# Moving the load of the norm factors ahead on ScalarE's DMA queue, and the first weight tile to SP's

## The chip, the cores and the metric

The kernel runs on one core of a Trainium2 chip. The time is that of the device, in microseconds (us), from several executions; each kernel is also profiled once, and the profile covers the span from the first to the last instruction of that execution.

The engines appear by the profile's names: PE (TensorE, the matmuls; PEld is its weight load), DVE (VectorE), ACT (ScalarE), POOL (GpSimd) and SP (SyncE, which here issues transfers only). A suffix q (ACTq, SPq) means the instruction stream of that engine in which transfers are issued.

## The reference

One layer of a decoder for 1024 tokens of width 1024, in float32:

```
u    = rms_norm(x, norm1_g)
proj = u @ w_in                       # q, k, v of 8 attention heads; q, f, i, g of 4 recurrent heads
attn = rms_norm(dilated_attention(q, k, v), attn_norm_g)
rec  = rms_norm(hgrn2_mixer(hq, hf, hi, lower_bound), hgrn_norm_g) * silu(hg)
h    = x + concat(attn, rec) @ w_out
u    = rms_norm(h, norm2_g)
gate, val = split(u @ w_up)
h    = h + (gelu(causal_conv3(gate)) * val) @ w_down
out  = rms_norm(h, final_norm_g)
```

where `rms_norm(x, g) = x * rsqrt(mean(x*x) + 1e-6) * g`. Only the first line and the columns of `w_in` for v matter to the change.

## The kernel before, in words

**Data and precision.** x is held transposed, channels on the 128 partitions: eight blocks c of 128 channels, each in two halves of 512 tokens. A matmul operand is split in two parts, a high one (the value rounded to a shorter format) and a low one (the rest), and each product is made of three matmuls: high times high, high times low, low times high. The norm's factor `g` is multiplied into x while it is split; the factor that belongs to the token is applied afterwards to the products.

**vec.** All per-channel vectors (norm factors, gate bounds, convolution weights and biases, 128 columns in all) come in one transfer of 64 KB into the tile `vec`, one channel to a partition. `col(j)` is a column of it. Columns 0 to 7 hold the factors of the first norm.

**The first stage (lines 573 to 592).** It computes v for all tokens into eight PSUM banks `V`. For each channel block c, `load_x` transfers the two halves of x (SP's queue, 256 KB each), `ring.fill(1)` transfers and splits the next weight tile, `scale_x` splits x times `col(V_G1 + c)` into a high part (on ACT, line 435) and a low part (on DVE, line 436), and `tok_step` issues 24 matmuls: for each of eight token blocks high x times high w (line 545), high x times low w (line 546) and low x times high w (line 550). The operands of the first block are called `B11h`, `B11l` (first half of the tokens) and `T4h`, `T4l` (second half; the name is of their later contents, in the same buffers).

**The weight ring.** `Ring.fill` takes the next entry of a plan, issues its transfer into a raw tile (`raww`, five of them) through the entry's `load` function, splits it into `whi` (line 89) and `wlo` (line 91, on DVE) and keeps up to five split tiles. Before the change, the `load` of the token weights (`tok`) issued on whatever queue `ring.queue` named: SP's, except for the very first tile, for which it was set to ACT's. The engine for `whi` is named by `ring.high`: ACT, except for the very first tile, which DVE splits in both parts.

**Order.** PE's instructions are issued in the order of the program. The others are ordered by a planner when the program is built, by its own estimates of time, except those wrapped in `pin` (`tc.keep_in_program_order`), which stay in the order in which they are written. In the first stage all loads and splits are pinned; from line 619 on the ring's are not. Before the first real matmul, `busy(9)` lets PE run matmuls of a tile of ones (`warm`, line 419), and the third matmul of the first token block is preceded by one more (`busy(1)`).

**The instructions that the change touches**, as they stood: the first block of x on SP's queue; the first weight tile on ACT's queue; behind it on ACT's queue the transfer of `vec`; then the load of ACT's table of functions (`preload_act_table_set`); then the first `scale_x`, which needs `vec` and the block of x.

Of the kernel before, what the change touches and what calls it, by code (L numbers as in the profile page):

```python
# [44 lines left out]
def f32(ap):  # L45
    return ap.bitcast(F32)


class Ring:


    def __init__(self, nc, pool, plan, tag="w", raws=5, depth=5, low=None):
        self.nc, self.pool, self.tag = nc, pool, tag
        self.RAWS, self.DEPTH, self.low = raws, depth, low or nc.vector
        self.plan, self.at, self.live, self.n = list(plan), 0, {}, 0
        self.raws = 0
        self.aside = {}
        self.step = 99
        self.on_vector = ()
        self.order = self.pin = lambda ins: ins  # L60
        self.high = nc.scalar.copy
        self.queue = nc.sync

    def raw(self, src=None):
        t = self.pool.tile([P, H2], F32, tag=f"raw{self.tag}", name=f"raw{self.tag}{self.raws}", bufs=self.RAWS)
# [186 lines left out]
def hybrid_kernel(ctx: ExitStack, tc: tile.TileContext, xT, w_qk, w_tok, w_hg, w_out, w_up,  # L252
                  w_down, vecs, amask, hmask, out):
    nc = tc.nc
    PE, DVE, ACT, POOL = nc.tensor, nc.vector, nc.scalar, nc.gpsimd
# [6 lines left out]
    ringp = ctx.enter_context(pool("ring", "left"))  # L262

    vec = cpool.tile([P, V_N], F32, name="vec")
    ones_r = cpool.tile([P, P], F32R, name="ones")
    ones = f32(ones_r)

# [26 lines left out]
    def tok(m, kh, c):  # L294

        def load(ring):
            t = ring.raw()
            w = w_tok[2 * m : 2 * m + 2, kh, :, c * 256 : (c + 1) * 256]
            ring.order(ring.queue.dma_start(t.rearrange("p (g n) -> p g n", g=2), w.rearrange("g p n -> p g n")))
            return t  # L300
        return load

# [35 lines left out]
    ring = Ring(nc, ringp, plan)  # L338
# [84 lines left out]
    pin = tc.keep_in_program_order  # L423
# [5 lines left out]
    def load_x(hf, c):  # L429
        pin(nc.sync.dma_start(xt[hf, c], xT[c, :, halves[hf]]))  # L430

    def scale_x(hf, c):
        hi, lo = (x[:, c % KS] for x in opn[OPS1[2 * hf + c // KS]])
        g = col(V_G1 + c)
        pin(ACT.mul(hi, xt[hf, c], g))
        pin(DVE.scalar_tensor_tensor(lo, xt[hf, c], g, f32(hi), op0=ALU.mult, op1=ALU.subtract))
# [137 lines left out]
    ring.step = 0  # L574
    V = [bank(x, f"v{t}") for t, x in enumerate("oottss")]
    load_x(0, 0)
    ring.high, ring.queue = DVE.tensor_copy, nc.scalar
    ring.fill(1)
    ring.high, ring.queue = ACT.copy, nc.sync
    pin(nc.scalar.dma_start(vec, vecs))  # L580
    pin(ACT.preload_act_table_set("natural_log_exp_and_others"))
    scale_x(0, 0)
    for c in range(NCT):
        if c:
# [1055 lines left out]
```

## Time and profile before

| | |
|---|---|
| Time, median of 3 runs | 1146.88 us (1146.65 to 1148.97) |
| The profiled execution: its time | 1147.14 us |
| Its span | 1145.4 us |
| PE busy | 1131.1 us (99%), 6416 matmuls |
| DVE busy | 959.7 us (84%) |
| ACT busy | 586.6 us (51%) |
| POOL busy | 88.2 us (8%) |
| Mean granted clock of PE | 0.997 |
| Data moved | 129.84 MB, mean 113 GB/s |

How to read it: a row of an engine's timeline is the start and the duration in us, the engine, the line, the operation and what it writes and reads (output <- inputs), with how many instructions the row merges (x) and, in square brackets, how long the engine stood idle before it and what ended that. An `ACTq` or `SPq` row is the issue of a transfer, which occupies the issuing engine only; when the data has landed stands in the list of transfers, as KB each and median us from issue to landing. In the list of waits, a row is "engine, line <- what it waited for: us in total, times, longest". In the windows view a row gives a stretch and its length, then for PE, PEld, DVE, ACT and POOL the busy time and the number of instructions, then the granted clock, the DMA share and GB/s.

### The profile page before, as it was taken

How to read it: one execution, taken by the hardware profiler on the slowest of the kernel's cores; microseconds unless marked ns; L12 is line 12 of the kernel's file. 1: busy time of each engine (PE TensorE's matmuls, PEld its weight loads, DVE VectorE, ACT ScalarE, POOL GpSimd, SP SyncE). 2: the span in 40 equal slices, each digit the busy share in tenths (PEclk: the TensorE clock that was granted, in tenths of full speed). 3: DMA queues.
4: the chain of work that ended last, by engine and by line, in shares of the span. 5: the costliest groups of instructions: out<-in, count | busy, mean ns of one | idle time of the engine just before them, and what ended most of it. 6: DMA issues, size and time to landing. Idle time of an engine off the chain costs nothing.

```text
span 1145.4 us, 17931 instructions
## 1 busy us (share of the span) xinstructions
PE 1131.1 (99%) x6416; PEld 928.9 (81%) x6416; DVE 959.7 (84%) x1748; ACT 586.6 (51%) x1177; POOL 88.2 (8%) x107
## 2 busy tenths in 40 slices
PE   9999999999999999999999999999999999999996
PEld 7887777778888888878788888888888888888885
DVE  7676877778999975889999989888988789857987
ACT  6544445465787875555433434343434354444553
POOL 5200233330000002000000000000000000000000
PEclk9999999999999999999999999999999999999998
DMA  7135221224313543221233223322332376335432
GB/s 250 59 99 152 64 76 58 84 75 161 116 59 102 174 129 101 84 65 46 74 111 117 87 100 129 111 82 95 126 111 83 117 267 230 116 98 175 157 120 74
DMA packets 98633, 129.84 MB, mean 113 GB/s; under 512 B 25008, under 2 KB 44240, under 8 KB 98544
## 3 DMA queue, kind: packets, MB, share of 16 engines
q1 hardware_dynamic: 83984, 103.77, 29.2%
q10 hardware_dynamic: 14560, 24.94, 5.8%
q8 instruction: 50, 0.82, 0.3%
q14 instruction: 39, 0.32, 0.1%
HBM read 97.58 MB, written 31.09 MB: 112 GB/s over the span
## 4 chain that ended last, share of the span: by engine, by line
PE 90%; DVE 7%; issue 1%; ACT 1%; DMA 1%; ACTq 0%; DVEq 0%; SPq 0%
PE p L1241 11%; PE p L1239 11%; PE p L1240 11%; PE w L491 5%; PE w L493 5%; PE w L492 5%; PE ds L1540 3%; PE ds L1538 3%; PE ds L1539 3%; PE da L1540 2%; PE da L1538 2%; PE da L1539 2%; PE po L491 2%; PE po L493 2%; PE po L492 2%; PE S L711 2%
## 5 line engine op out<-in xcount | busy, mean ns | idle before, releaser
L89 ACT CAST whi<-raww 128x512 fp32r<-128x512 f32 x257 | 157.3, 617 | 217.9 <-PE p L1240 74.0
L91 DVE TENSOR_TENSOR wlo<-raww,whi 128x512 fp32r<-128x512 f32 x258 | 179.8, 699 | 29.9 <-ACT whi L89 27.9
L89 ACT CAST whi<-r 128x512 fp32r<-128x512 f32 x70 | 43.6, 623 | 83.8 <-PE ds L1539 49.3
L91 DVE TENSOR_TENSOR wlo<-r,whi 128x512 fp32r<-128x512 f32 x70 | 47.9, 685 | 19.3 <-ACT whi L89 18.7
L1538 PE MATMUL ds<-fhi,whi 128*128 128x512 f32 x160 | 62.3, 389 | 0.0
L1540 PE MATMUL ds<-fhi,wlo 128*128 128x512 f32 x160 | 62.2, 389 | 0.0
L1239 PE MATMUL p<-b1h,whi 128*128 128x512 f32 x160 | 62.2, 389 | 0.0
L1240 PE MATMUL p<-b1l,whi 128*128 128x512 f32 x160 | 62.2, 389 | 0.0
L1241 PE MATMUL p<-b1h,wlo 128*128 128x512 f32 x160 | 62.2, 389 | 0.0
L1539 PE MATMUL ds<-flo,whi 128*128 128x512 f32 x160 | 62.2, 389 | 0.0
L724 POOL TENSOR_SCALAR P<-P,st 128x128 f32<-128x128 f32 (+7 forms) x64 | 46.5, 734 | 99.0 <-DVE st L723 91.9
L1512 POOL TENSOR_TENSOR facc<-facc,sqf 128x256 f32<-128x256 f32 x2 | 1.5, 740 | 674.0 <-ACT sqf L1511 674.0
L91 DVE TENSOR_TENSOR flo<-rawf,fhi 128x512 fp32r<-128x512 f32 x70 | 47.9, 684 | 3.2 <-ACT fhi L89 3.2
L89 ACT CAST fhi<-rawf 128x512 fp32r<-128x512 f32 x70 | 43.2, 617 | 13.4 <-PE p L1241 5.0
L722 ACT ACTIVATE P<-P,st 128x128 f32<-128x128 f32 (+7 forms) x64 | 35.7, 559 | 27.5 <-DVE st L720 27.5
L1268 ACT ACTIVATE cv<-cv 128x512 f32<-128x512 f32 x44 | 27.8, 632 | 41.0 <-DVE cv L1261 41.0
L1261 DVE SCALAR_TENSOR_TENSOR cv<-g,vec,cv 128x511 f32<-128x511 f32 (+2 forms) x92 | 44.6, 490 | 3.6 <-ACT cv L1258 3.3
L1538 PE MATMUL da<-fhi,whi 128*128 128x512 f32 x120 | 46.7, 389 | 0.0
L1539 PE MATMUL da<-flo,whi 128*128 128x512 f32 x120 | 46.7, 389 | 0.0
L1540 PE MATMUL da<-fhi,wlo 128*128 128x512 f32 x120 | 46.7, 389 | 0.0
L720 DVE CUSTOM_DVE_ANT_0 P<-S,mask 128x128 f32<-128x128 f32 (+7 forms) x64 | 28.9, 487 | 10.0 <-PE S L713 7.5
L1539 PEld LDWEIGHTS ds<-flo,whi 128*128 128x128 f32 x160 | 30.0, 188 | 6.3
(622 smaller groups left out, 3405.4 us busy)
## 6 DMA issues: line engine op xcount, KB each, us to landing
raww<-in_w_up_dram SPq DMA_DIRECT2D x88, 256.0 KB, 2.9
rawf<-spT SPq DMA_DIRECT2D x40, 256.0 KB, 2.8
r<-in_w_down_dram SPq DMA_DIRECT2D x40, 256.0 KB, 3.4
spB<-a ACTq DMA_DIRECT2D x30, 256.0 KB, 2.2
spT<-t ACTq DMA_DIRECT2D x30, 256.0 KB, 2.2
rawf<-spB SPq DMA_DIRECT2D x30, 256.0 KB, 2.7
raww<-in_w_out_dram SPq DMA_DIRECT2D x28, 256.0 KB, 2.8
raww<-in_w_hg_dram SPq DMA_DIRECT2D x24, 256.0 KB, 2.6
```

The source lines that it names most:

```text
L89: self.pin(self.high(hi[:, :w], raw))
L91: self.pin(low.tensor_sub(lo[:, :w], raw, f32(hi[:, :w])))
L491: PE.matmul(ps, a[0], b[0], start=start, stop=False)
L492: PE.matmul(ps, a[0], b[1], start=False, stop=False)
L493: PE.matmul(ps, a[1], b[0], start=False, stop=stop)
L724: POOL.tensor_scalar(Pt[:, :n], Pt[:, :n], st[:, 3:4], 1.0, op0=ALU.mult, op1=ALU.mult)
L1239: PE.matmul(ps, hi[:, s], bhi, start=(start and n == 0), stop=False)
L1240: PE.matmul(ps, hi[:, s], blo, start=False, stop=False)
L1241: PE.matmul(ps, lo[:, s], bhi, start=False, stop=(stop and n == len(rhs) - 1))
L1538: PE.matmul(ps[d], hi[:, s], ahi, start=(k == 0), stop=False)
L1539: PE.matmul(ps[d], hi[:, s], alo, start=False, stop=False)
L1540: PE.matmul(ps[d], lo[:, s], ahi, start=False, stop=(k == NPAIR - 1))
```

## The change

`vec`'s transfer is issued right where its tile is made, ahead of everything else in the kernel, on ACT's queue, and the table load right behind it. Neither is wrapped in `pin` any more. The first weight tile is issued by SP like all others, as SP's second transfer, behind the first block of x and ahead of that block's second half; `ring.queue` is gone. DVE still splits the first weight tile.

```diff
@@ Ring.__init__
         self.high = nc.scalar.copy
-        self.queue = nc.sync
@@ hybrid_kernel
     vec = cpool.tile([P, V_N], F32, name="vec")
+    nc.scalar.dma_start(vec, vecs)
+    ACT.preload_act_table_set("natural_log_exp_and_others")
     ones_r = cpool.tile([P, P], F32R, name="ones")
@@ tok.load
-            ring.order(ring.queue.dma_start(t.rearrange("p (g n) -> p g n", g=2), w.rearrange("g p n -> p g n")))
+            ring.order(nc.sync.dma_start(t.rearrange("p (g n) -> p g n", g=2), w.rearrange("g p n -> p g n")))
@@ first stage
     load_x(0, 0)
-    ring.high, ring.queue = DVE.tensor_copy, nc.scalar
+    ring.high = DVE.tensor_copy
     ring.fill(1)
-    ring.high, ring.queue = ACT.copy, nc.sync
-    pin(nc.scalar.dma_start(vec, vecs))
-    pin(ACT.preload_act_table_set("natural_log_exp_and_others"))
+    ring.high = ACT.copy
     scale_x(0, 0)
```

## The prediction

> **What bounds the kernel now.** I read the page first, then PE's waits, then the first microseconds engine by engine, because the change touches only loads issued before the first real matmul. On the page, each engine row gives busy time, share of the span and number of instructions.
>
> ```profile
> span 1145.4 us, 17931 instructions
> ...
> PE 1131.1 (99%) x6416; PEld 928.9 (81%) x6416; DVE 959.7 (84%) x1748; ACT 586.6 (51%) x1177; POOL 88.2 (8%) x107
> ```
>
> PE is the bound: it is idle for 1145.4 - 1131.1 = 14.3 us in all. The list of who waited for whom, PE's rows alone, says where anything at all holds it up (total, times, longest):
>
> ```profile
> PE v L545 <- ACT B11h L435: 1.2, 1, 1.2
> PE warm L419 <- DVE eps L280: 1.1, 1, 1.1
> PE w L491 <- DVE G L529: 0.8, 1, 0.8
> PE p0g L1239 <- DVE h L1134: 0.8, 1, 0.8
> PE w L491 <- DVE u L522: 0.5, 1, 0.5
> PE p L1241 <- DVE wlo L91: 0.3, 1, 0.3
> ```
>
> The longest is the first real matmul, which waits for B11h, the scaled first block of x. The chain of waits followed back from the end begins with exactly that:
>
> ```profile
> 1.22 4.30 DMA vec<-in_vecs_dram
> 5.61 0.73 ACT B11h L435
> ```
>
> So the kernel's start is set by vec, the vector of norm factors: issued at 1.22, landed at 1.22 + 4.30 = 5.52, and B11h begins 0.09 later. Behind that start PE is hardly ever let go; the windows view of everything from 50 to 1100 us (length, then PE busy) shows it:
>
> ```profile
> 50.00:1100.00 1050.00, 1047.48 (x6006) 857.91 (x6005) 889.74 (x1636) 538.67 (x1089) 63.41 (x85) 1.00 0.35 111
> ```
>
> Only 2.5 us of 1050 are idle. A microsecond saved ahead of the first matmul is therefore carried to the end, as one lost there would be; and no more can be won by this change than the start holds.
>
> **The start, engine by engine.** ScalarE, with the DMA issues of its queue (ACTq):
>
> ```profile
> 0.73 0.46 ACTq L299 DMA_DIRECT2D raww<-in_w_tok_dram  x1
> 1.22 0.48 ACTq L580 DMA_DIRECT2D vec<-in_vecs_dram  x1
> 1.74 1.28 ACT L581 ACT_TABLE_LOAD   x1 [1.74 <-issue]
> 5.61 0.72 ACT L435 ACTIVATE B11h<-xs_qp,vec 128x512 fp32r<-128x512 f32 x1 [2.59 <-DMA vec<-in_vecs_dram]
> ```
>
> VectorE, from the split of the first weight tile (whi, then wlo) to the low parts of x and the second weight tile:
>
> ```profile
> 4.63 0.43 DVE L89 CAST whi<-raww 128x512 fp32r<-128x512 f32 x1 [3.60 <-DMA raww<-in_w_tok_dram]
> 5.09 0.69 DVE L91 TENSOR_TENSOR wlo<-raww,whi 128x512 fp32r<-128x512 f32 x1
> 6.36 0.75 DVE L436 SCALAR_TENSOR_TENSOR B11l<-xs_qp,vec,B11h 128x512 fp32r<-128x512 f32 x1 [0.58 <-ACT B11h L435]
> 7.03 0.74 DVE L436 SCALAR_TENSOR_TENSOR T4l<-xs_qp,vec,T4h 128x512 fp32r<-128x512 f32 x1
> 7.82 0.69 DVE L91 TENSOR_TENSOR wlo<-raww,whi 128x512 fp32r<-128x512 f32 x1
> 8.45 0.75 DVE L436 SCALAR_TENSOR_TENSOR B11l<-xs_qp,vec,B11h 128x512 fp32r<-128x512 f32 x1
> ```
>
> And PE:
>
> ```profile
> 1.05 4.09 PE L419 MATMUL warm<-ones 128*128 128x128 f32 x18 [1.05 <-DVE eps L280]
> 6.38 0.50 PE L545 MATMUL v<-whi,B11h 128*128 128x512 f32 x1 [1.24 <-ACT B11h L435]
> ...
> 7.17 0.50 PE L550 MATMUL v<-whi,B11l 128*128 128x512 f32 x1
> ...
> 12.29 0.39 PE L545 MATMUL v<-whi,B11h 128*128 128x512 f32 x1
> ```
>
> The reader should see two inputs that meet. PE's first matmul needs whi and B11h; its third (L550, 7.17) needs B11l. From that third one on PE does not stop again. B11l stands behind whi and wlo on VectorE and needs B11h from ScalarE; it started at 6.36, when B11h was there, after VectorE had stood idle for 0.58. So two loads decide when L550 can go: vec, through B11h, and the first weight tile (w0 below), through whi and wlo. The change brings one forward and puts the other back.
>
> **What it removes, adds and moves.** No instruction is added or taken away: the same transfers, the same table load, the same arithmetic.
>
> *Vec becomes the first transfer of ScalarE's queue.* Its issue moves from 1.22 to 0.73, 0.49 earlier, and it no longer has w0's 256 KB ahead of it on that queue. The rows of transfers that bear on its time (KB each, then us from issue to landing) are those issued at 0.73 on ScalarE's queue and at 0.74 on SP's, and a 64 KB load from much later:
>
> ```profile
> raww<-in_w_tok_dram ACTq DMA_DIRECT2D x1, 256.0 KB, 3.9
> xs_qp<-in_xT_dram SPq DMA_DIRECT2D x1, 256.0 KB, 3.3
> ...
> near<-vd SPq DMA_DIRECT2D x32, 64.0 KB, 2.1
> ```
>
> Vec's time is at least the 2.1 of the small load and at most the 4.3 it has now. I take 3.3: first on its queue, it starts beside SP's first block of x and is smaller. It then lands at 0.73 + 3.3 = 4.03 (2.83 to 5.03). B11h also needs that block of x, which landed at 0.74 + 3.3 = 4.04. So B11h starts at 4.04 + 0.09 = 4.13 instead of 5.61 and ends at 4.85.
>
> *The table load* goes with it, from 1.74 to about 1.25, and ends at 2.53, long before B11h: it costs nothing. Without that cover it would cost 1.28, but ScalarE stands idle for 2.59 there.
>
> *w0 moves to SP's queue, as its second transfer.* SP's queue so far:
>
> ```profile
> 0.74 1.34 SPq L430 DMA_DIRECT2D xs_qp<-in_xT_dram  x3
> 2.13 0.43 SPq L299 DMA_DIRECT2D raww<-in_w_tok_dram  x1
> ```
>
> Three issues took 1.34, one about 0.45, so w0 is issued at 1.19 instead of 0.73, and all that follows on SP (two blocks of x, the second weight tile, and so on) 0.45 later. Two rows price the place: SP's second transfer of now, and the first weight tile that SP loads.
>
> ```profile
> xs_qp<-in_xT_dram SPq DMA_DIRECT2D x1, 256.0 KB, 4.1
> ...
> raww<-in_w_tok_dram SPq DMA_DIRECT2D x1, 256.0 KB, 5.0
> ```
>
> SP's second transfer landed at 1.19 + 4.1 = 5.29, but by then w0 (landed at 4.63) had come in too: three loads of 256 KB. With the change, only the first x block, vec and w0 have to be through: 256 + 64 + 256 KB, 192 KB (0.197 MB) less. The rate at that time:
>
> ```profile
> 3.30:5.30 2.00, 1.84 (x10) 1.65 (x8) 0.63 (x2) 0.00 (x0) 0.00 (x0) 1.00 1.08 351
> ```
>
> 351 GB/s makes 0.56 us of that, so I estimate 5.29 - 0.56 = 4.73, a tenth later than now. The bounds: 1.19 + 3.3 = 4.49 (as the first x block) and 5.29 (as SP's second now).
>
> [...]
>
> *Then the sum.* From w0's landing: whi to wlo is 5.09 - 4.63 = 0.46; wlo to a B11l that is not waiting is 8.45 - 7.82 = 0.63. So B11l starts at 4.73 + 0.46 + 0.63 = 5.82. B11h (4.85) is no longer what it waits for: the wait passes from vec to w0. That is 6.36 - 5.82 = 0.54 earlier, and L550 moves from 7.17 to 6.63. The two matmuls and the short warm pair ahead of it fit: the first starts at about 5.2 when whi is there, L546 at 5.9 after wlo. The warming matmuls end at 1.05 + 4.09 = 5.14, so the hole of 1.24 before the first matmul nearly closes; the granted clock in the rows of this time is 1.00 already, so I give nothing for it.
>
> *What is put back on SP* costs nothing. The second weight tile was split by 7.82 + 0.69 = 8.51 and is first used at 12.29. Even 0.54 earlier in use and 0.45 later in landing leaves 2.8 us of cover; beyond that each microsecond would cost one. The second x block, later by an issue, feeds T4l, due on PE after four token blocks of three matmuls, past 9 us.
>
> The gain is 0.54 us: against the profiled execution, 1147.14 us with a span of 1145.4 (1.74 lies around it), 1146.60. The median of the three runs shown is 1146.88, 0.26 below that execution, so the forecast of the median is 1146.34, in round terms 1146.3. By the bounds of w0 alone B11l starts between 5.58 (gain 0.78, 1146.1) and 6.38 (loss 0.02, 1146.9). At vec's bound of 5.03 B11h ends at 5.03 + 0.09 + 0.72 = 5.84, which is no later than B11l's turn.
>
> **The rivals.**
>
> *Only the issue times move.* If the transfers share the engines as before, whatever the queue, vec lands 0.49 earlier, at 5.03, and w0 an issue later, at 4.63 + 0.46 = 5.09. B11l then starts at 5.09 + 1.09 = 6.18, a gain of 0.18: 1146.7. For it speaks that the DMA engines were full (share 1.08 in the row above); against it, that vec would still need 4.3 us with nothing ahead of it on its queue. [...]
>
> *w0 is late: slower.* If the weight tile behaves on SP's queue as the first weight tile that SP loads now, it takes 5.0, lands at 6.19, and B11l starts at 7.28: 0.92 later, 1147.8. The place is VectorE's cast at L89, and from 5.27 on (6.36 - 1.09) it decides for slower. For it: that row is the same kind of transfer on the same queue. Against: that one was fourth in line, not second.
>
> *The order of instructions changes.* The transfer and the table load of the change are no longer pinned in program order, and from line 619 on most work is not pinned either; a planner orders it at build time by its own times. If a shift of those times at the start swaps neighbours later, PE gains or loses waits. The rows price one at 0.3 to 0.8. Three new ones of 0.8, say where L491 and L1239 already wait for VectorE, are 2.4 us: with the 0.54 won, 1148.7; one more passes 0.2%. All four waits after the start gone (0.8 + 0.8 + 0.5 + 0.3 = 2.4) would make 1143.9. For it: VectorE is busy 84% and near ties abound. Against: PE's own order is fixed by hand, and PE's start shifts everything behind it alike.
>
> **How the numbers follow.** The forecast (gain 0.0 to 0.8) gets 0.56, issue times only 0.14, w0 late 0.10, another order 0.20. No change of the first three moves the time by 0.2% (2.3 us, about what a measurement of this kernel can tell from none), but for 0.01 of w0 late, beyond its row. The last is split 0.08 faster, 0.03 within, 0.09 slower. So faster 0.08, same 0.56 + 0.14 + 0.09 + 0.03 = 0.82, slower 0.10. The likeliest case's own range is 1146.1 to 1146.9, but the runs of one kernel spread by 2.3 us (1146.65 to 1148.97), and another order reaches 2.4 to either side: 1144.2 to 1148.7 leaves out about 2 in 10.
>
> **What would show it.** Right: the chain no longer begins with vec but with w0; B11h starts near 4.1, whi at 4.5 to 5.3, L550 near 6.6; PE's 1.2 us wait is gone or small and is put down to VectorE or w0; PE rows after 50 us are the same, half a microsecond earlier. Wrong: vec landing after 5.0 (issue times only); whi later than 5.27 (loss); PE waits after 50 us that are not in the list above, or other neighbours on VectorE (order). The time itself can hardly tell the first three apart, the start of L550 can.

## The result, and the profile after

| | before | changed |
|---|---|---|
| median of 21 executions each | 1147.0 us | 1146.18 us |
| lowest to highest | 1146.65 to 1148.97 | 1145.99 to 1146.80 |
| profiled execution, its time and span | 1147.14, 1145.4 | 1146.05, 1144.3 |

The ratio is 0.9988 (95% interval 0.9983 to 0.9994). By the 0.2% that the prediction took as the bound of what can be told, that is the same time; yet the whole interval lies below 1, so a small gain is clear. One execution of a kernel further down (vec first only), of 2038.11 us at a granted clock of 0.725, is left out of its ratio. Two things lie in the ratio here. Before, 14 of 21 executions lie at 1146.65 to 1147.18 (median 1146.93) and seven at 1148.31 to 1148.97; the changed kernel has one group only. So its gain is 0.75 us against the lower group of before, and 1.8 more in each execution that would have fallen in the upper one. The first part is of the kind that was predicted; the second was not.

The page of the changed kernel, span and engines:

```profile
span 1144.3 us, 17931 instructions
...
PE 1131.4 (99%) x6416; PEld 929.1 (81%) x6416; DVE 959.4 (84%) x1748; ACT 587.1 (51%) x1177; POOL 88.3 (8%) x107
```

The chain that ended last, at its beginning (start, length, what):

```profile
0.74 0.40 SPq L431
1.19 3.31 DMA raww<-in_w_tok_dram
4.53 0.44 DVE whi L88
4.99 0.70 DVE wlo L90
```

It no longer begins with vec but with the first weight tile on SP's queue, and goes on through VectorE. The transfers of the start (KB, us to landing):

```profile
xs_qp<-in_xT_dram SPq DMA_DIRECT2D x1, 256.0 KB, 3.0
raww<-in_w_tok_dram SPq DMA_DIRECT2D x1, 256.0 KB, 3.3
vec<-in_vecs_dram ACTq DMA_DIRECT2D x1, 64.0 KB, 3.2
```

The timelines of ScalarE, of VectorE and of PE:

```profile
0.73 0.42 ACTq L264 DMA_DIRECT2D vec<-in_vecs_dram  x1
1.18 1.28 ACT L265 ACT_TABLE_LOAD   x1 [1.18 <-PEq L1627]
3.92 0.72 ACT L436 ACTIVATE B11h<-xs_qp,vec 128x512 fp32r<-128x512 f32 x1 [1.46 <-DMA vec<-in_vecs_dram]
...
4.53 0.43 DVE L88 CAST whi<-raww 128x512 fp32r<-128x512 f32 x1 [3.50 <-DMA raww<-in_w_tok_dram]
4.99 0.69 DVE L90 TENSOR_TENSOR wlo<-raww,whi 128x512 fp32r<-128x512 f32 x1
5.59 0.75 DVE L437 SCALAR_TENSOR_TENSOR B11l<-xs_qp,vec,B11h 128x512 fp32r<-128x512 f32 x1
...
1.05 4.17 PE L420 MATMUL warm<-ones 128*128 128x128 f32 x18 [1.05 <-DVE eps L281]
5.10 0.47 PE L546 MATMUL v<-whi,B11h 128*128 128x512 f32 x1
5.73 0.50 PE L547 MATMUL v<-wlo,B11h 128*128 128x512 f32 x1 [0.17 <-DVE wlo L90]
...
6.40 0.50 PE L551 MATMUL v<-whi,B11l 128*128 128x512 f32 x1
```

(The third matmul is on L551 here, and still called L550 below.) Vec landed at 0.73 + 3.2 = 3.93 instead of 5.52, and B11h starts at 3.92 (landings are rounded to 0.1). VectorE runs whi, wlo and B11l without a hole, B11l at 5.59 instead of 6.36, and L550 starts at 6.40 instead of 7.17: 0.77 earlier. The hole of 1.24 between the warming and the first real matmul is gone. PE's waits, all of them:

```profile
PE warm L420 <- DVE eps L281: 1.1, 1, 1.1
PE w L492 <- DVE G L530: 0.9, 1, 0.9
PE p0g L1238 <- DVE h L1133: 0.8, 1, 0.8
PE w L492 <- DVE u L523: 0.3, 1, 0.3
PE v L547 <- DVE wlo L90: 0.2, 1, 0.2
```

Those at G, h and u are as before within 0.2, and the 0.3 at L1241 is gone; the 1.2 for B11h has become 0.2 for wlo.

### The profile page after: what moved, and what is told of

The parts are those of the page before. It is cut to its first block, busy times and chain, and to the rows that moved or that the text cites. A ratio compares the mean times of both kernels' runs of the same rounds, so it can differ in the third digit from the quotient of the medians.

```text
span 1144.3 us, 17931 instructions
## 1 busy us (share of the span) xinstructions
PE 1131.4 (99%) x6416; PEld 929.1 (81%) x6416; DVE 959.4 (84%) x1748; ACT 587.1 (51%) x1177; POOL 88.3 (8%) x107
## 4 chain that ended last, share of the span: by engine, by line
PE 91%; DVE 7%; issue 1%; DMA 1%; ACT 0%; DVEq 0%; SPq 0%; ACTq 0%
PE p L1240 11%; PE p L1239 11%; PE p L1238 11%; PE w L492 5%; PE w L494 5%; PE w L493 5%; PE ds L1537 3%; PE ds L1539 3%; PE ds L1538 3%; PE da L1537 2%; PE da L1539 2%; PE da L1538 2%; PE po L492 2%; PE po L494 2%; PE po L493 2%; PE S L710 2%
## 5 line engine op out<-in xcount | busy, mean ns | idle before, releaser
L1539 PEld LDWEIGHTS ds<-fhi,wlo 128*128 128x128 f32 x160 | 30.0, 188 | 6.3
```

Of the source, the lines that this page charges most:

```text
L1539: PE.matmul(ps[d], lo[:, s], ahi, start=False, stop=(k == NPAIR - 1))
```

## The experiments

**Is it carried to the end?** Across the profiled executions of all kernels, the span less the start of L550 tells. "Hole" is PE's idle time ahead of the first real matmul.

| profiled execution | hole | L550 | span | span - L550 |
|---|---|---|---|---|
| before | 1.24 | 7.17 | 1145.4 | 1138.2 |
| before, three more | 1.64, 1.36, 1.22 | 7.11, 6.94, 7.02 | 1144.9, 1144.9, 1144.8 | 1137.8, 1138.0, 1137.8 |
| vec first only | 0.65 | 7.09 | 1144.9 | 1137.8 |
| before, 12 warming calls | 0.70 | 7.85 | 1145.8 | 1138.0 |
| before, 15 warming calls | 0 | 7.99 | 1147.1 | 1139.1 |
| changed, twice | 0, 0 | 6.40, 6.63 | 1144.3, 1144.5 | 1137.9, 1137.9 |
| changed, 6 warming calls, twice | 1.21, 0.98 | 6.49, 6.47 | 1144.6, 1145.6 | 1138.1, 1139.1 |
| w0 before x | 0.46 | 6.51 | 1145.1 | 1138.6 |
| w0 fourth | 1.76 | 8.31 | 1147.8 | 1139.5 |
| w0 fourth, 13 warming calls | 1.16 | 8.96 | 1147.0 | 1138.0 |

Ten of fourteen lie within 1137.8 to 1138.2, though L550 itself moves from 6.40 to 8.96: the start is carried to the end one to one. The other four lose something more behind L550, which is looked for below.

**Vec first, w0 behind it on the same queue.** This is the change without its other half (against the kernel of before; only the lines that matter).

```diff
+    nc.scalar.dma_start(vec, vecs)          # where vec's tile is made
     ...
     load_x(0, 0)
     ring.high, ring.queue = DVE.tensor_copy, nc.scalar
     ring.fill(1)
     ring.high, ring.queue = ACT.copy, nc.sync
-    pin(nc.scalar.dma_start(vec, vecs))
     pin(ACT.preload_act_table_set("natural_log_exp_and_others"))
```

> Only half of the change: vec is the first transfer of ScalarE's queue, the first weight tile w0 stays on that queue as its second, issued at about 1.2. Theory (w0 gains by having SP's line to itself behind one x block, and L550's start is carried to the end one to one): here w0 shares the engines in turns with SP's x blocks as before and lands one issue later than before, 4.63 + 0.45 = 5.1; third matmul (L550) at about 7.0, some 0.2 ahead of before and 0.6 behind the changed kernel; time 0.2 below before, 0.6 above the changed kernel. Rival (what counts is when a load is issued, not on whose queue): w0, issued at 1.2 as in the changed kernel, lands at 4.5 as there; L550 at 6.4 and the time of the changed kernel.

VectorE's timeline of it, where the first weight tile arrives:

```profile
5.22 0.43 DVE L89 CAST whi<-raww 128x512 fp32r<-128x512 f32 x1 [4.19 <-DMA raww<-in_w_tok_dram]
5.68 0.69 DVE L91 TENSOR_TENSOR wlo<-raww,whi 128x512 fp32r<-128x512 f32 x1
```

Issued at 1.17, hardly earlier than in the changed kernel (1.19), w0 was there at 5.2 and not at 4.5. So it does matter on whose queue it stands, and the rival is out. (That the two queues share the engines, as the theory has it, is in the trace of before: from 3.0 to 3.5 us the 43 packets of SP's queue took 41.9% of the 16 engines' time and the 108 of ScalarE's 62.8%.) L550 started at 7.09, where the theory had 7.0. The ratio was 0.9997 (0.9988 to 1.0006): vec alone, 1.6 us earlier, won nothing that can be measured, because the wait passes to w0, which itself came 0.6 later than before. Two of its ten executions lie at 1148.46 and 1148.95, so the upper group is not gone either. The other half alone was not run: with w0 on SP's queue and vec's two lines left where they were, vec would be the first on ScalarE's queue anyway, and every engine should have the same instructions in the same order as in the changed kernel. By that argument the move of w0 is the change.

**w0 ahead of x on SP's queue** (against the changed kernel).

```diff
-    load_x(0, 0)
     ring.high = DVE.tensor_copy
     ring.fill(1)
     ring.high = ACT.copy
+    load_x(0, 0)
```

> The changed kernel with w0 ahead of the first x block on SP's queue. Theory (L550 waits for the later of two chains, w0 -> whi -> wlo -> B11l and x -> B11h -> B11l): w0 lands at about 3.8, x at 4.5; B11h from 4.6 to 5.3, B11l from about 5.35 instead of 5.59, L550 at 6.1 to 6.2 instead of 6.40; time 0.2 to 0.3 below the changed kernel. Rival (x behind 1 KB rows comes as late as SP's third transfer in the changed kernel, 5.1): B11l from 5.9, L550 at 6.7, 0.3 slower than the changed kernel.

The first rows of ScalarE, VectorE and PE after the loads:

```profile
4.95 0.72 ACT L436 ACTIVATE B11h<-xs_qp,vec 128x512 fp32r<-128x512 f32 x1 [2.44 <-DMA xs_qp<-in_xT_dram]
...
5.70 0.75 DVE L437 SCALAR_TENSOR_TENSOR B11l<-xs_qp,vec,B11h 128x512 fp32r<-128x512 f32 x1 [0.29 <-ACT B11h L436]
...
6.51 0.50 PE L551 MATMUL v<-whi,B11l 128*128 128x512 f32 x1
```

x came at 4.9, between the two expectations, and w0 at 4.26 and not at 3.8. B11l now waits 0.29 for B11h: the wait went back to the other chain. L550 at 6.51 is between the two figures that the changed kernel itself shows (6.40 and 6.63), and the ratio to before is 0.9988 (0.9979 to 0.9996), the same as the change's. Ten of its 11 executions lie at 1145.81 to 1146.90, one at 1148.02. Its time can't be told from the changed kernel's; of the two loads that are needed, one has to be second.

**w0 as SP's fourth transfer.** The three x blocks that were first are issued ahead of it (against the changed kernel; the loop below no longer issues these three, which is not shown).

```diff
-    load_x(0, 0)
+    for hf, c in ((0, 0), (1, 0), (0, 1)):
+        load_x(hf, c)
     ring.high = DVE.tensor_copy
     ring.fill(1)
```

> The changed kernel with w0 as SP's fourth transfer, behind three x blocks. Theory (the start of L550 is carried to the end one to one): w0 lands where SP's fourth transfer lands in the changed kernel, about 7.2 instead of 4.5; L550 at about 9.1 instead of 6.4; time 2.7 above the changed kernel, about 1148.9. Rival 1 (slack later on takes up the start): L550 as late, the time less than 1 above. Rival 2 (PE, idle from 5.2 to 7.7, is granted a lower clock and loses more): more than 3.5 above.

w0 was there at 6.44, earlier than the 7.2 expected, and L550 at 8.31 is 1.91 after that of the changed kernel. The median of 1150.5 is 4.2 to 4.3 above the changed kernel's two medians (1146.18 and 1146.29; ratio to before 1.0025, 1.0015 to 1.0034). So neither the one-to-one theory alone nor rival 1 holds, and rival 2 does. Where the extra loss lies stands in PE's rows and in the windows view (length, then PE busy; the third number from the end is the granted clock):

```profile
8.65 0.43 PE L546 MATMUL v<-whi,B11h 128*128 128x512 f32 x1
8.89 0.62 PE L547 MATMUL v<-wlo,B11h 128*128 128x512 f32 x1
9.31 0.63 PE L551 MATMUL v<-whi,B11l 128*128 128x512 f32 x1
...
12.29 0.40 PE L546 MATMUL v<-whi,T4h 128*128 128x512 f32 x1
12.53 0.39 PE L547 MATMUL v<-wlo,T4h 128*128 128x512 f32 x1
...
5.30:8.60 3.30, 1.41 (x5) 0.96 (x6) 2.12 (x4) 1.42 (x3) 0.00 (x0) 1.00 1.04 348
8.60:12.20 3.60, 3.60 (x10) 2.84 (x10) 3.60 (x7) 3.60 (x7) 0.00 (x0) 0.54 1.03 365
```

For 3.3 us around the hole PE was busy 1.41 only; for some 3.4 us after that the matmuls start 0.42 apart, not 0.23, and the granted clock is 0.54 over 3.6 us. By estimate from these rows, half a clock for 3.4 us loses 1.7 us, close to the 1.6 by which this row of the table stands off 1137.9. The profiled execution took 1149.65, the fastest of its nine; the median lies 0.85 higher. The mean granted clock, which is on record for every execution here, splits the nine: a stretch of 3.4 us at half should take 0.0015 off it (1.7 of 1148), and the four that read 0.995 or 0.996, this one among them, took 1149.65 to 1150.35, while the five at 0.997 or 0.998 took 1150.50 to 1151.15. The five lose more although no such drop shows in them; where is the question of the last experiment. In this trace the clock record has the half rate from 8.88 to 12.29, for 3.41 us; it begins 1.86 after the end of the hole (7.02), and PE had not been idle in between but for the 0.17 ahead of L547. Why the clock drops there, these rows do not show.

**The upper group of before.** The unchanged kernel again:

> The kernel of before, unchanged. Its 21 executions beside the changed kernel lie in two groups, 14 at 1146.65 to 1147.18 and 7 at 1148.31 to 1148.97; the changed kernel's 21 all lie at 1145.99 to 1146.80. If the upper group belongs to the order of loads at its start, about one in three executions lies near 1148.7 here too; if it came from the chip that these runs had, none or all.

Three of 11 lay at 1148.46 to 1148.70. Over all of the record, on several chips, 44 of 111 executions of before lie at 1148.13 or more (two of them at 1150.2), the others at 1147.54 or less; of the changed kernel, none of 32 lies above 1146.80. So it belongs to the program. The hole of before is 1.2 to 1.6 us long in its profiles, that of the changed kernel nil, and the distance of the groups is the 1.7 estimated for the slow stretch of w0 fourth. Four kernels change the hole and leave the loads alone, by one number in `busy(9)`. First, the hole put into the changed kernel, `busy(6)`:

> The changed kernel with 6 warming calls instead of 9, so that PE stands idle from about 3.9 to 5.1 ahead of the first real matmul; loads and L550 (6.4) as in the changed kernel. Theory (the clock): an upper group appears, about one execution in three at 1147.7 to 1148.2, the others at 1146.0 to 1146.6. Rival (the loads, not the hole, made the upper group): all at 1146.0 to 1146.8.

Its PE rows:

```profile
1.05 2.93 PE L420 MATMUL warm<-ones 128*128 128x128 f32 x12 [1.05 <-DVE eps L281]
5.19 0.47 PE L546 MATMUL v<-whi,B11h 128*128 128x512 f32 x1 [1.21 <-DVE whi L88]
```

Eight of 11 executions lie at 1147.74 to 1148.57, where one in three was expected, and three at 1146.10 to 1146.38; the ratio to before is 1.0003 (0.9994 to 1.0012). With the loads of the change and L550 where the change puts it, the hole and three warming calls fewer take all of the gain away. Beside it ran the changed kernel as it is:

> The changed kernel once more, on the chip of the other three, for comparison. Both theories: 1146.0 to 1146.8, without an upper group.

1146.09 to 1146.69, all 11; ratio 0.9989 (0.9980 to 0.9998).

Second, the hole of before filled, with 12 and then with 15 calls:

> The kernel of before with 12 warming calls instead of 9, so that PE works until about 6.1 instead of 4.7 to 5.1; loads and their order as before, L550 at 7.1 as before. Theory (the clock: the hole of 1.2 to 1.6 us ahead of the first real matmul lets PE's granted clock fall to half for 3.4 us in some executions, which costs some 1.7 us, as the row of the kernel with w0 fourth shows): the upper group of before, near 1148.6, is gone; all executions at 1146.5 to 1147.2. Rival (the upper group comes from the loads or from later on): it stays, about one execution in three.

> The kernel of before with 15 warming calls instead of 9: PE works until about 7.2, past the latest start of the first real matmul seen so far (7.07), so that no hole is left in any execution. Theory (the clock): no upper group at all; the executions lie in one group, later than the lower group of before by what the warming now delays the first matmul, 0.1 to 0.9: 1146.9 to 1147.8. Rival (the upper group comes from the loads or from later on): about one execution in three 1.7 above the others.

With 12, two of 11 stay in the upper group (1148.30, 1148.47), and the profiled execution still shows a hole of 0.70, since vec came later in it and B11h with it. That is fewer than the 13 of 33 of before on that chip, but 11 executions are too few to call it shown. With 15 there is no hole and no second group 1.7 above the rest: ten lie at 1148.04 to 1148.90, one at 1147.36. But the ten lie 0.2 or more later than expected, and so where the upper group of before lies; the ratio to before is 1.0006 (0.9997 to 1.0015). The times alone therefore do not decide between theory and rival. In the profiled execution L550 started at 7.99, 0.8 to 1.05 after that of before and so at the far end of what the theory allowed for, and PE has a new wait:

```profile
PE w L491 <- DVE E L525: 0.9, 1, 0.9
```

It stands at about 305 us, in the middle of the kernel, and the kernel with w0 before x has the same one with 0.6. With it two more of the four odd rows of the table are explained in the main (1139.1 and 1138.6). VectorE's order of instructions is the same; that a shift of a few tenths at the start decides whether it comes too late there is likely, but not shown. How often it does so, the few profiles don't tell.

Third, 13 calls in the kernel with w0 fourth:

> The kernel with w0 as SP's fourth transfer, with 13 warming calls instead of 9, so that PE works until w0 is split, about 7.0; L550 at 8.3 as without them. Theory (start carried one to one, and the rest of its loss is the clock): 1.9 above the changed kernel, about 1148.1, and the granted clock 1.00 from 8 to 13 us. Rival (the loss comes from the late loads further on): 1150 as without them.

Eight of 11 lie at 1148.27 to 1149.08, three at 1150.06 to 1150.39, where without the calls all nine lay at 1149.65 to 1151.15. The profiled execution has the clock at 1.00 from 8 to 13 us (behind L550 its matmuls start 0.23 to 0.24 apart) and a span less L550 of 1138.0: the late loads cost nothing further on, and the loss was the clock's. w0 came later in it (7.1 us), so 1.16 of the hole was left, and with it, it seems, the three.

Last, profiles for the upper group itself:

> The changed kernel with 6 warming calls once more, for a profile: 8 of its 11 executions lay near 1148. Theory (the clock): in a profiled execution of the upper group the granted clock is 0.50 for about 3.4 us soon after the first real matmul, some 8 matmuls of the first channel block take 0.43 from start to start instead of 0.23, and everything behind is 1.7 later. Rival: clock 1.00 throughout, and the 1.7 lie elsewhere.

> The kernel of before, for a profile of an execution of its upper group (about 4 in 10). Theory (the clock): if the execution takes over 1148, the granted clock is 0.50 for about 3.4 us between 6 and 13 us, as in the kernel with w0 fourth; if it takes under 1147.5, the clock is 1.00 there. Rival: clock 1.00 there in both.

> The same as the one before it, once more: over 1148 with the clock at 0.50 for 3.4 us between 6 and 13 us, or under 1147.5 with 1.00. Rival: clock 1.00 there in both.

Both of before took under 1147.5 (1146.75 and 1146.62), with the clock at 1.00; none of its upper executions has been profiled. The one with 6 warming calls took 1147.36, between its groups, and fits neither its theory nor its rival. Its PE rows, and the windows row for them:

```profile
6.47 0.78 PE L551 MATMUL v<-whi,B11l 128*128 128x512 f32 x1
7.05 0.63 PE L546 MATMUL v<-whi,B11h 128*128 128x512 f32 x1
7.47 0.63 PE L547 MATMUL v<-wlo,B11h 128*128 128x512 f32 x1
...
8.76 0.52 PE L547 MATMUL v<-wlo,B11h 128*128 128x512 f32 x1
9.12 0.40 PE L551 MATMUL v<-whi,B11l 128*128 128x512 f32 x1
9.35 0.40 PE L546 MATMUL v<-whi,B11h 128*128 128x512 f32 x1
...
5.00:9.00 4.00, 4.00 (x10) 3.05 (x11) 2.19 (x4) 1.60 (x3) 0.00 (x0) 1.00 0.97 343
```

The matmuls after L550 start 0.43 apart until about 8.8 and 0.23 after 9.1, while the column of the granted clock says 1.00. The trace explains the column: its clock record begins only at 9.03, and the view prints 1.00 where there is no record. So in this execution PE ran at half rate until 9.03, came up late, and lost 1.2 (1139.1 against 1137.9). The second profile of the changed kernel shows the same on a small scale, with a record that begins at 6.52:

```profile
5.23 0.77 PE L546 MATMUL v<-whi,B11h 128*128 128x512 f32 x1
5.86 0.79 PE L547 MATMUL v<-wlo,B11h 128*128 128x512 f32 x1
6.63 0.48 PE L551 MATMUL v<-whi,B11l 128*128 128x512 f32 x1
```

In the four profiles of before the record begins at 3.94, 4.17, 4.63 and 4.89, and the 18 warming matmuls take 3.64, 3.75, 3.97 and 4.09; where it begins only after them (5.47, 5.66 and 6.52, in three kernels with 9 calls) they take 4.21. So in these traces the start of the record is the moment at which PE speeds up, and it varies between executions, from 3.94 to 9.03. The three calls fewer are not the whole reason for the late one: in the first profile with 6 calls, after the same 2.93 us of warming, the record begins at 4.08.

The profiles thus have two ways to lose time, a clock that drops after a hole (w0 fourth, half rate from 8.88 to 12.29) and a clock that comes up late (6 calls, at 9.03), and only the first shows in the mean granted clock (0.996, against 0.997). The upper group of before is hardly the first: of its 44 executions 37 have their mean clock on record, 32 at 0.997 and five at 0.998, and the 53 lower ones read the same (45 and eight), where such a drop would take off the estimated 0.0015. A clock that comes up 3.4 us late would, by the same estimate, cost the 1.7 us, and leave the mean alone as it did with 6 calls. No upper execution of before has been profiled, so this is argued and not shown, and a wait in the middle of the kernel, like the 0.9 at E, is not excluded.

## Why the prediction was right, and what it missed

- *What bounds the start* held: two loads meet in B11l, the wait passed from vec to w0, and whi, wlo and B11l ran back to back.
- *Vec* was to land at 4.03 and B11h to start at 4.13; it was 3.93 and 3.92. (One reading of the sum is off by a hair: at vec's bound of 5.03, B11h's end at 5.84 is 0.02 after B11l's turn at 5.82, and not ahead of it. Nothing hung on it.) The rival that only issue times move (vec at 5.03, w0 at 5.09) is refuted, by the landing and by the kernel with vec first only.
- *w0* was the term that was mis-sized: put at 4.73, between bounds of 4.49 and 5.29, it landed at 1.19 + 3.3 = 4.5, at the lower bound. The estimate subtracted bytes from a row in which ScalarE's queue was also full; with that queue empty but for vec, SP's second transfer took hardly longer than its first (3.3 and 3.0). The gain at L550 was 0.77 instead of 0.54, and the lower groups differ by 0.75.
- *The sum* was carried through as argued: the table's last column. The load put back on SP's queue cost nothing, as was said: ScalarE took the second weight tile at 8.05, VectorE had it split at 9.40, and PE waits for neither.
- *w0 late* did not come, but the kernel with w0 fourth shows that the place and the direction were right; the price there was 1.91 for the start and 1.7 more for the clock.
- *Another order* did not come either: on every engine the instructions stand as before, but for the one transfer that moved from ScalarE's queue to SP's.
- The step that failed is the sentence on the hole: "the granted clock in the rows of this time is 1.00 already, so I give nothing for it". It read one execution, of the lower group, and a column that prints 1.00 where the trace has no record; in that very trace the record begins at 4.89. Putting the hole into the changed kernel, by three warming calls fewer, took the whole gain away in eight of 11 executions (1.45 to 2.28 above the changed kernel's 1146.29, with a hole of 1.21 in the profile), so such a hole can cost more than its length; if the upper group of before is the hole's, it was worth 1.8 us in about four executions of ten.
- Part of the agreement is luck. The forecast of 1146.3 started from the median of three executions, two of which happened to lie in the lower group; with two of them in the upper one it would have started near 1148.7. The range was widened for the scatter of before without asking for its source, though the measured 1146.18 lies also in the narrower 1146.1 to 1146.9.
- That the upper group of before comes from the start and the clock is supported by the hole put in, by the group's distance and by the profile in which the clock came up late. The hole filled does not add much: two of 11 stayed with 12 calls, and with 15 the later start and the wait at E hide what it may have won.

## What to carry to other kernels

When two loads meet ahead of the first matmul, price both chains and give each load a queue position for itself: advancing the one that is waited for is worth only the distance to the other, here nothing measurable until w0 was moved too. Executions that fall in two groups ask for a look at the hole between warming matmuls and real work, since a hole that the profiled execution survives may cost others more than its length (with 6 calls the profiled one, with a hole of 1.21, took 1146.35, eight others 1147.74 to 1148.57). Judge PE's speed at the start of a kernel by the distance from one matmul's start to the next: the clock column said 1.00 before its first record (9.03) while the matmuls started 0.43 apart.

## What the runs showed of the hardware

- In the profile of w0 fourth PE had a hole of 1.76 (5.26 to 7.02) and ran at half rate from 8.88 to 12.29, 3.41 us (starts 0.42 to 0.43 apart against 0.23, granted clock 0.54 from 8.60 to 12.20), at a price of 1.6 us by the table, 1.7 by estimate. The mean granted clock of that kernel is lower, 0.995 or 0.996, in four of nine executions; in before, with holes of 1.2 to 1.6 in its profiles, it reads 0.997 or more in all 90 on record.
- The time at which PE came up to full rate at the start of a kernel varied between the profiled executions, from 3.94 us after the first instruction (a profile of before) to 9.03 (the second with 6 calls). In the latter the 512-column matmuls started 0.43 apart until then where they followed each other, and 0.23 after, and the granted clock in the profile printed 1.00 throughout.
- In the changed kernel w0, behind one 256 KB block on SP's queue and with 64 KB alone on the other, took 3.3 us (issued at 1.19, there at 4.5). In the kernel with vec first only, issued at 1.17 behind those 64 KB and against three blocks of x on SP's queue, it was there at 5.2, 0.7 later.
- Landings differed between executions: w0 as SP's fourth transfer was there at 6.44 in the profile with 9 warming calls and at 7.1 in that with 13, on another chip.
